# Hybrid encoder layer on one core: the up-projection's weight sums formed during the mixers' projection, three more activations fetched ahead of each down stage, and some transfers kept in program order

## The chip, the cores and the metric

The kernel runs on one core of a Trainium2 chip. The metric is device time in microseconds (us) of one execution; the time before is the median of three runs. Beside it stands one execution that the hardware profiler recorded. A core has TensorE (PE, matmuls, with PEld for its weight loads), VectorE (DVE), ScalarE (ACT), GpSimd (POOL) and SyncE (SP), which here issues nearly all transfers. Each engine works through its own instructions in order; semaphores tie them together.

## The reference, cut to what matters

One layer is computed for a prompt of 2048 rows and for 8 sample sequences of 16 rows (128 rows), with D = 1024:

```python
h = rms_norm(x, norm_g[0])
z = h @ w_in                                  # 1024 x 3592
att = rms_norm(band_attention(qa, ka, va), g_att)         # 8 heads of 64
mem = sigmoid(ob) * head_norm(mlstm(qb, kb, vb, ib, fb))  # 4 heads of 128
x = x + rms_norm(concat(att, mem) @ w_out, norm_g[1])
u = rms_norm(x, norm_g[2]) @ w_up             # 1024 x 5632
y = causal_depthwise_conv(u, width=3)
ffn = (gelu(y[:, :2816]) * y[:, 2816:]) @ w_down          # 2816 x 1024
x = x + rms_norm(ffn, norm_g[3])
```

All is float32. Outputs are x and the caches and states of both request groups.

## The kernel before, in words

Every float32 product is made of three matmuls (`mm3`, L95 to L97) on operands that ScalarE and VectorE split into a high part (a cast) and a low part (a subtraction). The rows form 17 tiles of 128: 16 of the prompt and one of all samples (SAMPLE).

**The mixers' projection** goes over the tiles twice, as two halves of 9 and 8 tiles. In each half 14 groups of columns of w_in (`GROUPS`, gi = 0 to 13) are multiplied; `group_T` yields after every four of eight k steps (12 steps per group), `group_rows` likewise (two steps per tile: 18 or 16). The loop at L1186 takes these steps one by one. In each it also takes a step of whatever else is under way, loads and splits of the next group's weights (`load_group`), norms of input rows (`norm_steps`), and calls `pump`, which steps two pipes of units: attention heads and mLSTM heads. [...] The tag "grow" of the pool `const` has one buffer, which holds the input norm's row during the projection, the mix norm's row (`norm_row(1)`) during the output projection, and later the last norm's row.

**The output projection** (`project`) follows, and from tile 8 on the FFN's pools are open.

**The FFN** runs over three blocks of 6, 6 and 5 tiles (`FBLOCKS`, L1387). Its up-projection is a Strassen-Winograd scheme: for each f of 22 (128 gate and 128 up columns), seven products of quarter matrices (`product`, L1395), 84 matmuls. Four of the seven weight operands are sums of the quarters a11, a12, a22 and a21. In block 0, `load_quads` (L1255) loads the four quarters of an f (L1262), forms four sums on GpSimd (L1267, 128×512 each), stores them in DRAM as `wsd[f]` (L1269) and uses the tiles directly; blocks 1 and 2 load three quarters and four kept sums (L1278). `load_up` (L1282) splits each operand (`split`, L1250 and L1251). The raw tiles are "quads", 128×512, of which there are 11 buffers; w_down's raw tiles, the early activations and the `later` units below share them.

Per f the products' results leave PSUM through `x1` to `x3`, `uu` and `ug` (L1403, L1473 to L1492); `conv` makes the convolution with VectorE's L1423 and L1424, and the gated product is stored as `gd[b][f]` (L1501). `conv` and the product use three row buffers (`row`, tag "yq").

**The down stage** of a block goes twice over the 22 f, once per half `dh` of the output columns, here called k; each k has 18 (or 15) matmuls of 128×512. `fetch` (L1438) reads gd[b][k] back, into two quads if `early`, else into a row buffer (L1447); `split_g` (L1449) splits it into two of four "w3" tiles. Activations 0 and 1 are fetched early, at f = 20, and split at f = 21; from there on, each step k fetches k+1. In each step the pipe `ahead` takes a step: the next block's normed and transposed rows (`h2_units`) and the `later` units of the previous block's output tiles (L1353), which load a half row of the FFN's result and of x (L1357, L1358), scale, add and store.

Before block 0, `late_B` (L1131) loads and splits four of the seven row operands.

Of the kernel before, what the change touches and what calls it, by code (L numbers as in the profile page):

```python
# [17 lines left out]
P = 128  # L18
# [26 lines left out]
def hymba_step(ctx: ExitStack, tc: tile.TileContext, I: dict, O: dict):  # L45
# [1085 lines left out]
    def late_B():  # L1131

        for i in (P5, P2, P4, P3):
# [3 lines left out]
            nc.scalar.copy(hi, lo.bitcast(F32))  # L1137
            nc.vector.tensor_tensor(lo, lo.bitcast(F32), hi, op=ALU.subtract)  # L1138

    GROUPS = ["va0", "qk0", "qk1", "va1", "qk2", "qk3", "qb0", "vo0", "qb1", "vo1", "qb2", "vo2", "qb3", "vo3"]  # L1140
    SRC = {g: i for i, g in enumerate(["va0", "qk0", "qk1", "va1", "qk2", "qk3",
                                       "qb0", "vo0", "qb1", "vo1", "qb2", "vo2", "qb3", "vo3"])}
# [24 lines left out]
    def norm_steps(half):  # L1167

        for ci, tiles in enumerate(HALVES[half]):
            ch = phT.tile([P, 2, KT, 384], F32R, tag="hT", name=f"hT{half}_{ci}", bufs=3)  # L1170
            chunks.append(ch)
            for j, t in enumerate(tiles):
                norm_tile(t, ch, j, ps_big)
                yield 0.9, 2.5
# [3 lines left out]
    pipes += [Pipe(att_stream()), Pipe(mem_stream())]  # L1178
    chunks = []
    norms = norm_steps(0)  # L1180
    next(norms)
    pend = load_group(0)
    for _ in pend[2]:
# [2 lines left out]
    for n_, (half, gi) in enumerate(seq):  # L1186
        wh, wl, _ = pend
        split = iter([])
        if n_ + 1 < len(seq):
            pend = load_group(seq[n_ + 1][1])  # L1190
            split = pend[2]
        g = GROUPS[gi]
        i = int(g[2])
        nm = f"{g}_{half}"
        if g[:2] == "va":
            it = group_rows(wh, wl, half, chunks, vd[i], nm, 264 if gi == 0 else 256,
                            [O["v_prompt"][i], O["v_sample"][i].unsqueeze(1)])
        elif g[:2] == "qk":
            it = group_T(wh, wl, half, chunks, [qTd[i], kTd[i]], [-(DA ** -0.5), None], nm,
                         [None, [O["k_prompt"][i], O["k_sample"][i]]])  # L1200
        elif g[:2] == "qb":
            it = group_T(wh, wl, half, chunks, [[t_[:, c, :] for t_ in qkbd[i]] for c in range(2)],
                         [None, DH ** -0.5], nm)
        else:
            it = group_rows(wh, wl, half, chunks, vobd[i], nm)
        if half == 0 and gi == 13:
            chunks = []
            norms = norm_steps(1)
        if n_ == len(seq) - 1:
            out = project([0, 1, 2, 3, 4, 5, 6, 7, SAMPLE, 8, 9, 10, 11, 12, 13, 14, 15])  # L1210
            split = w_out_steps()
            next(split)
            next(out)
        for u, (pe, dve) in enumerate(it):
            ahead = []
            if n_ < len(seq) - 1 or u >= 6:
                ahead.append(next(split, (0.0, 0.0)))
            if n_ == len(seq) - 1 and u == 12:
                ahead.append(next(out))
            if (half == 0 and gi == 13 and u >= 6 and u % 2 == 0) or (gi == 0 and u % 2 == 0):  # L1220
                ahead.append(next(norms, (0.0, 0.0)))
            pump(pe + sum(a[0] for a in ahead), dve + sum(a[1] for a in ahead))
        for _ in split:
            pass
        if gi == 0:
            if half == 0:
                nc.sync.dma_start(bgate, I["b_gate"].broadcast_to([P, 8]))
                nc.sync.dma_start(gatt, I["g_att"])
                heads.append(build_bias)
                mems.append(lambda: prep(prep_sample()))  # L1230
            mems.append(lambda half=half: prep(prep_prompt(half)))
        if g[:2] == "qk":
            attention(i, half)
            if half == 0 and i == 3:
                heads.insert(len(heads) % 4, lambda: attention_sample(0, EARLY))
            if half == 1 and i == 0:
                heads.insert(len(heads) % 4, lambda: attention_sample(EARLY, DB))
        if g[:2] == "vo":
            mems.append(lambda i=i, half=half: mlstm(i, half))
            if half == 0:  # L1240
                mems.append(lambda i=i: mlstm_sample(i))
# [8 lines left out]
        nc.scalar.copy(h, r)  # L1250
        nc.vector.tensor_tensor(l, r, h, op=ALU.subtract)  # L1251

    raws = {}

    def load_quads(b, f, g):  # L1255

        src = lambda i: I["w_up"][f][:, i * 512:(i + 1) * 512]
        if b == 0 and g == 0:
            q = []
            for i in range(4):  # L1260
                q.append(quad(f"wu{f}_{i}"))
                nc.sync.dma_start(q[i], src(i))  # L1262
            a11, a12, a22, a21 = q
            s1, s2, s3, s4 = [quad(f"ws{f}_{i}") for i in range(4)]
            for o, x, y, op in ((s1, a21, a22, ALU.add), (s2, s1, a11, ALU.subtract), (s3, a11, a21, ALU.subtract),
                                (s4, a12, s2, ALU.subtract)):
                nc.gpsimd.tensor_tensor(o, x, y, op=op)  # L1267
            for i, o in enumerate((s2, s3, s1, s4)):
                nc.sync.dma_start(wsd[f][:, i * 512:(i + 1) * 512], o)  # L1269
            raws[f] = [a12, a22, s4]  # L1270
            return [a11, s2, s3, s1]
        if b == 0:
            return raws.pop(f)
        kept = lambda i: wsd[f][:, i * 512:(i + 1) * 512]
        out = []
        for i, s_ in enumerate([[src(0), kept(0), kept(1), kept(2)], [src(1), src(2), kept(3)]][g]):
            r = quad(f"wu{b}_{f}_{g}_{i}")
            nc.sync.dma_start(r, s_)  # L1278
            out.append(r)
        return out  # L1280
# [72 lines left out]
    def later(t, rs):  # L1353

        def unit(half):
            v, x, c = quad(f"f{half}{t}"), quad(f"x{half}{t}"), half * 512
            nc.sync.dma_start(v, (f0d, f1d)[half][t])  # L1357
            nc.sync.dma_start(x, x2d[t][:, c:c + 512])  # L1358
            yield 0.0, 0.0
            nc.vector.scalar_tensor_tensor(v, v, rs, g3[:, c:c + 512], op0=ALU.mult, op1=ALU.mult)  # L1360
            nc.gpsimd.tensor_tensor(v, v, x, op=ALU.add)
            nc.sync.dma_start(out_rows(t)[:, c:c + 512], v)
            yield 0.0, 1.0

        return [unit(half) for half in range(2)]
# [21 lines left out]
    for b, tiles in enumerate(FBLOCKS):  # L1387
# [48 lines left out]
        n2 = nt * P // 2  # L1436

        def fetch(dh, k, early=False):  # L1438
            if k >= NF:
                return  # L1440
            if early:
                g[dh, k] = [quad(f"gr{b}_{dh}_{k}_{i}")[:, :n2] for i in range(2)]
                for i, r in enumerate(g[dh, k]):
                    nc.sync.dma_start(r, gd[b][k][:, i * n2:(i + 1) * n2])
            else:
                g[dh, k] = row(f"gr{b}_{dh}_{k}")
                nc.sync.dma_start(g[dh, k][:, :2 * n2], gd[b][k][:, :2 * n2])  # L1447
# [14 lines left out]
        for f in range(NF):  # L1462
# [20 lines left out]
            if f == NF - 1:  # L1483
                split_g(0, 0, w3_tile)
                split_g(0, 1, w3_tile)
            ug = u_tile(f"ug{nm}")
            product(P2, w[0], a, onto=True)
            nc.scalar.copy(ug[:, 2:2 + n], a[:, :n])
# [18 lines left out]
        for dh in range(2):  # L1507
# [9 lines left out]
            for c in range(6):  # L1517
# [16 lines left out]
                if tail and c >= 4:  # L1534
                    places = []
                    for i in ((0, 1) if c == 4 else (2,)):
                        t_ = p3.tile([P, 2, 4, 384], F32R, tag=f"B{i}", name=f"gtail{i}", bufs=1)
                        t_ = t_.rearrange("p a k n -> p (a k n)")
                        places += [t_[:, x * 768:(x + 1) * 768] for x in range(4)]
                    for k in ks:  # L1540
                        split_g(dh, k, lambda name: places.pop())
                        fetch(dh, k + 1)
                    if c == 4:
                        wh4, wl4 = wh, wl
                        continue
                    for j in range(nt):
                        for k in range(16, 20):
                            down(j, k, wh4, wl4)
                        for k in ks:
                            down(j, k, wh, wl)  # L1550
                        finish(b, j, load_rest(b, j), *evacuate(b, j, accs[j], 1), res[j])
                    continue
                for k in ks:
                    if (dh, k) not in parts:
                        split_g(dh, k, w3_tile)
                    if k + 1 == NF and dh == 0:
                        fetch(1, 0)
                    elif dh == 1 or k >= 1:
                        fetch(dh, k + 1)
                    for j in order if k == NF - 1 else range(nt):  # L1560
                        down(j, k, wh, wl)
                    if k >= 1:
                        ahead.step()
# [115 lines left out]
```

## Time and profile before

| | us |
|---|---|
| median of 3 runs | 2871.17 |
| lowest and highest | 2869.95, 2876.76 |
| profiled execution | 2872.21 |
| its span, first to last instruction | 2870.5 |

| busy in the span | us | share |
|---|---|---|
| PE | 2752.3 | 96% |
| PEld | 2566.0 | 89% |
| DVE | 1899.5 | 66% |
| ACT | 1405.6 | 49% |
| POOL | 561.8 | 20% |

How such lines are read: a group of instructions has its line in the kernel, the engine, the operation, the tiles written and read (out<-in), the shapes and the count; then busy time and the mean of one in ns; then the engine's idle time just before them and what ended it (the releaser). A row of waits has who waited for whom, the total in us, the number of times and the longest. A row of busy times by stretch has the stretch in us from the span's start, its length, the busy us and count of each engine, then PEclk (the granted TensorE clock, 1.00 is full), the DMA engines' busy share and GB/s. A row of the timeline has its start, its duration, the instruction, and in brackets the idle time before it and its releaser. Rows of DMA issues have the count, the size of one and the median time from issue to landing.

### The profile page before, as it was taken

Reading aid. Unit: us, or ns where it says so; the run is one execution under the profiler, and the core shown is the slowest. Engines: PE = TensorE matmul, PEld = TensorE weight load, DVE = VectorE, ACT = ScalarE, POOL = GpSimd, SP = SyncE. Lnnn points to the kernel's source line nnn. Section 1 sums busy time; section 2 is a strip of 40 time slices with the busy share of each in tenths; the row PEclk is TensorE's granted clock in tenths of the full one; section 3 lists DMA queues with packets and bytes.
Section 4 is the critical chain, followed back from the end, with each engine's and each line's share of the span. In section 5 each row is a group of like instructions: output and inputs, shape, how many; then the busy total and the mean of one; then the engine's idle time right before and its main releaser. Section 6 shows DMA issues by size and latency. Waiting matters only on the chain.

```text
span 2870.5 us, 47064 instructions
## 1 busy us (share of the span) xinstructions
PE 2752.3 (96%) x16587; PEld 2566.0 (89%) x16587; DVE 1899.5 (66%) x3345; ACT 1405.6 (49%) x2827; POOL 561.8 (20%) x964
## 2 busy tenths in 40 slices
PE   8899999999999999999999989999999899999898
PEld 7899989989899998878989978899999778999787
DVE  5344455645456678576999976467777754888755
ACT  4344555534356676343444445345554443555433
POOL 1000010211000003255555410011111210222311
PEclk9999999999999999999999999999999999999899
DMA  4544355556555564366444545645444775555766
GB/s 163 171 120 124 110 174 152 177 161 194 169 154 153 157 192 148 106 198 211 152 166 144 167 141 171 217 147 158 148 149 162 235 242 160 171 174 181 234 222 200
DMA packets 312122, 486.04 MB, mean 169 GB/s; under 512 B 55282, under 2 KB 148174, under 8 KB 311758
## 3 DMA queue, kind: packets, MB, share of 16 engines
q1 hardware_dynamic: 273294, 449.21, 50.1%
q10 hardware_dynamic: 38592, 33.83, 3.5%
q8 instruction: 130, 2.13, 0.3%
q14 instruction: 106, 0.87, 0.1%
HBM read 359.36 MB, written 126.70 MB: 169 GB/s over the span
## 4 chain that ended last, share of the span: by engine, by line
PE 49%; DVE 7%; issue 2%; DMA 2%; ACT 1%; POOL 1%; SPq 0%; DVEq 0%; ACTq 0%; POOLq 0%
PE uec L95 5%; PE uec L96 5%; PE uec L97 5%; PE dn L97 4%; PE dn L96 4%; PE dn L95 4%; PE ua L95 3%; PE ua L97 2%; PE ua L96 2%; PE dnm L95 2%; PE dnm L97 2%; PE dnm L96 2%; PE wo L97 2%; PE wo L95 2%; PE wo L96 2%
## 5 line engine op out<-in xcount | busy, mean ns | idle before, releaser
L95 PE MATMUL uec<-B,wuh 128*128 128x384 f32 (+1 forms) x720 | 236.2, 329 | 7.9 <-DVE uu L1490 7.9
L1251 DVE TENSOR_TENSOR gl<-gr,gh 128x768 fp32r<-128x768 f32 (+3 forms) x132 | 117.8, 897 | 188.2 <-ACT gh L1250 188.1
L96 PE MATMUL uec<-B,wuh 128*128 128x384 f32 (+1 forms) x720 | 235.6, 327 | 0.4 <-DVE B L1138 0.4
L97 PE MATMUL uec<-B,wul 128*128 128x384 f32 (+1 forms) x720 | 233.0, 327 | 0.0
L1250 ACT CAST gh<-gr 128x768 fp32r<-128x768 f32 (+3 forms) x132 | 101.5, 773 | 238.2 <-PE dn L96 200.0
L95 PE MATMUL dn<-wdh,gh 128*128 128x512 f32 x466 | 185.1, 397 | 7.9 <-DVE ug L1403 7.9
L96 PE MATMUL dn<-wdl,gh 128*128 128x512 f32 x466 | 185.9, 399 | 0.0
L1251 DVE TENSOR_TENSOR wul<-wu,wuh 128x512 fp32r<-128x512 f32 x255 | 179.3, 742 | 9.4 <-ACT wuh L1250 6.6
L1250 ACT CAST wuh<-wu 128x512 fp32r<-128x512 f32 x255 | 141.6, 617 | 71.3 <-PE uec L96 67.5
L97 PE MATMUL dn<-wdh,gl 128*128 128x512 f32 x466 | 170.4, 398 | 0.0
L96 PE MATMUL vo<-wi_l,hT 128*128 128x256 f32 x544 | 155.7, 286 | 0.0
L95 PE MATMUL vo<-wi_h,hT 128*128 128x256 f32 x544 | 154.9, 285 | 0.6 <-DVE mt L199 0.6
L97 PE MATMUL vo<-wi_h,hT 128*128 128x256 f32 x544 | 155.3, 285 | 0.0
L387 DVE CUSTOM_DVE_ANT_0 tmp<-s,nb 128x640 f32<-128x640 f32 (+4 forms) x128 | 94.3, 737 | 77.1 <-PE s L377 73.6
L95 PEld LDWEIGHTS uec<-B,wuh 128*128 128x128 f32 x720 | 135.4, 188 | 11.0 <-DVE uu L1490 9.8
L96 PEld LDWEIGHTS uec<-B,wuh 128*128 128x128 f32 x720 | 135.5, 188 | 0.9 <-DVE B L1138 0.7
L97 PEld LDWEIGHTS uec<-B,wul 128*128 128x128 f32 x720 | 135.1, 188 | 0.0
L95 PE MATMUL qk<-hT,wi_h 128*128 128x384 f32 (+1 forms) x384 | 128.8, 335 | 4.2 <-ACT qk_st L226 3.6
L95 PE MATMUL dnm<-wdh,gh 128*128 128x512 f32 x252 | 101.8, 407 | 31.6 <-ACT gh L1250 29.8
L388 ACT ACTIVATE tmp<-tmp,mn 128x640 f32<-128x640 f32 (+4 forms) x128 | 97.6, 762 | 70.2 <-DVE mn L387 65.9
L400 DVE TENSOR_TENSOR ptl<-pt,pth 128x640 fp32r<-128x640 f32 (+4 forms) x128 | 93.5, 737 | 55.8 <-ACT pth L399 54.7
L97 PE MATMUL qk<-hT,wi_l 128*128 128x384 f32 (+1 forms) x384 | 128.9, 336 | 0.0
(409 smaller groups left out, 9065.4 us busy)
## 6 DMA issues: line engine op xcount, KB each, us to landing
wu<-in_w_up SPq DMA_DIRECT2D x220, 256.0 KB, 3.8
wu<-wsd SPq DMA_DIRECT2D x176, 256.0 KB, 5.0
wdr<-in_w_down SPq DMA_DIRECT2D x132, 256.0 KB, 4.5
gr<-gd SPq DMA_DIRECT2D x84, 384.0 KB, 3.5
wi_raw<-in_w_in SPq DMA_DIRECT2D x52, 512.0 KB, 4.4
wsd<-ws SPq DMA_DIRECT2D x88, 256.0 KB, 3.2
gd<-g SPq DMA_DIRECT2D x44, 384.0 KB, 2.8
kraw<-kTd SPq DMA_DIRECT2D x112, 128.0 KB, 3.4
```

The source lines that it names most:

```text
L95: nc.tensor.matmul(out, ah, bh, start=start, stop=False, skip_group_check=onto)
L96: nc.tensor.matmul(out, ah, bl, start=False, stop=False, skip_group_check=onto)
L97: nc.tensor.matmul(out, al, bh, start=False, stop=stop, skip_group_check=onto)
L387: nc.vector.tensor_tensor_reduce(o_, s_, b_, 1.0, 3e38, ALU.add, ALU.min, accum_out=mn)
L388: nc.scalar.activation(tmp[:, :n], tmp[:, :n], AF.Exp, bias=mn, scale=-1.0, accum_out=rsum[:, i % 4, hh:hh + 1])
L400: nc.vector.tensor_tensor(s.ptl[:, sl, qc], ptv, s.pth[:, sl, qc], op=ALU.subtract)
L1250: nc.scalar.copy(h, r)
L1251: nc.vector.tensor_tensor(l, r, h, op=ALU.subtract)
```

## The change: what it does

1. **The sums.** `sum_steps` makes all 22 f's weight sums during the projection: 44 units, each of half the columns. A unit loads a 128×4×256 tile (512 KB) into the "grow" buffer, takes three steps, makes four additions in place on GpSimd (128×256), takes two steps, stores the tile into wsd, and takes two more. The loop takes one step of it in each step of groups 2 to 12 of the first half and 1 to 12 of the second; a unit under way is finished at the start of group 13. Its loads and stores go through `keep_in_program_order`, which puts an instruction behind the one traced before it on the same engine. As "grow" is needed by it, the input norm's row is loaded again for the second half (`g0.clear()`).
2. **The loads.** `load_quads` no longer forms sums: all three blocks load four and three quads per f, three quarters and four kept sums, in wsd's new order.
3. **The `later` units' loads** (L1357, L1358) are kept in program order too.
4. **Early fetches.** At f = 21 of every block, after activations 0 and 1 are split, activations 2, 3 and 4 are fetched early, into quads. From there on each step k of the down stage fetches k+2 instead of k+1, and the last steps of the first half fetch activations 0 and 1 of the second.

```diff
+    def sum_steps():
+        for f in range(NF):
+            for e in range(2):
+                view = lambda t: t.rearrange("p (q c) -> p q c", q=4)[:, :, e * 256:(e + 1) * 256]
+                w = const.tile([P, 4, 256], F32, tag="grow", name=f"ws{f}_{e}")
+                tc.keep_in_program_order(nc.sync.dma_start(w, view(I["w_up"][f])))
+                for _ in range(3):
+                    yield True
+                a11, a12, a22, a21 = [w[:, i] for i in range(4)]
+                nc.gpsimd.tensor_tensor(a22, a21, a22, op=ALU.add)
+                nc.gpsimd.tensor_tensor(a21, a11, a21, op=ALU.subtract)
+                nc.gpsimd.tensor_tensor(a11, a22, a11, op=ALU.subtract)
+                nc.gpsimd.tensor_tensor(a12, a12, a11, op=ALU.subtract)
+                for _ in range(2):
+                    yield True
+                tc.keep_in_program_order(nc.sync.dma_start(view(wsd[f]), w))
+                yield True
+                yield False
...
+    sums, under_way = sum_steps(), False
...
         if half == 0 and gi == 13:
             chunks = []
             norms = norm_steps(1)
+            g0.clear()
...
+            if 2 - half <= gi < 13:
+                under_way = next(sums, False)
+            while gi == 13 and under_way:
+                under_way = next(sums)
             pump(pe + sum(a[0] for a in ahead), dve + sum(a[1] for a in ahead))
...
-        src = lambda i: I["w_up"][f][:, i * 512:(i + 1) * 512]
-        if b == 0 and g == 0:
-            q = []
-            for i in range(4):
-                q.append(quad(f"wu{f}_{i}"))
-                nc.sync.dma_start(q[i], src(i))
-            a11, a12, a22, a21 = q
-            s1, s2, s3, s4 = [quad(f"ws{f}_{i}") for i in range(4)]
-            for o, x, y, op in ((s1, a21, a22, ALU.add), (s2, s1, a11, ALU.subtract), (s3, a11, a21, ALU.subtract),
-                                (s4, a12, s2, ALU.subtract)):
-                nc.gpsimd.tensor_tensor(o, x, y, op=op)
-            for i, o in enumerate((s2, s3, s1, s4)):
-                nc.sync.dma_start(wsd[f][:, i * 512:(i + 1) * 512], o)
-            raws[f] = [a12, a22, s4]
-            return [a11, s2, s3, s1]
-        if b == 0:
-            return raws.pop(f)
+        own = lambda i: I["w_up"][f][:, i * 512:(i + 1) * 512]
         kept = lambda i: wsd[f][:, i * 512:(i + 1) * 512]
         out = []
-        for i, s_ in enumerate([[src(0), kept(0), kept(1), kept(2)], [src(1), src(2), kept(3)]][g]):
+        for i, s_ in enumerate([[own(0), kept(0), kept(3), kept(2)], [own(1), own(2), kept(1)]][g]):
...
-            nc.sync.dma_start(v, (f0d, f1d)[half][t])
-            nc.sync.dma_start(x, x2d[t][:, c:c + 512])
+            tc.keep_in_program_order(nc.sync.dma_start(v, (f0d, f1d)[half][t]))
+            tc.keep_in_program_order(nc.sync.dma_start(x, x2d[t][:, c:c + 512]))
...
-            if k >= NF:
+            if dh > 1 or k >= NF:
...
                 split_g(0, 1, w3_tile)
+                for k in range(2, 5):
+                    fetch(0, k, True)
...
                         split_g(dh, k, lambda name: places.pop())
-                        fetch(dh, k + 1)
+                        fetch(dh, k + 2)
...
-                    if k + 1 == NF and dh == 0:
-                        fetch(1, 0)
-                    elif dh == 1 or k >= 1:
-                        fetch(dh, k + 1)
+                    if dh == 1 or k >= 3:
+                        fetch(dh + (k + 2) // NF, (k + 2) % NF)
```

More of the change, by code (lines that the diff above doesn't have):

```diff
@@ L1251, in split @@
         nc.vector.tensor_tensor(l, r, h, op=ALU.subtract)
-    raws = {}
     def load_quads(b, f, g):
-        src = lambda i: I["w_up"][f][:, i * 512:(i + 1) * 512]
-        if b == 0 and g == 0:
-            q = []
-            for i in range(4):
-                q.append(quad(f"wu{f}_{i}"))
-                nc.sync.dma_start(q[i], src(i))
-            a11, a12, a22, a21 = q
-            s1, s2, s3, s4 = [quad(f"ws{f}_{i}") for i in range(4)]
-            for o, x, y, op in ((s1, a21, a22, ALU.add), (s2, s1, a11, ALU.subtract), (s3, a11, a21, ALU.subtract),
-                                (s4, a12, s2, ALU.subtract)):
-                nc.gpsimd.tensor_tensor(o, x, y, op=op)
-            for i, o in enumerate((s2, s3, s1, s4)):
-                nc.sync.dma_start(wsd[f][:, i * 512:(i + 1) * 512], o)
-            raws[f] = [a12, a22, s4]
-            return [a11, s2, s3, s1]
-        if b == 0:
-            return raws.pop(f)
+        own = lambda i: I["w_up"][f][:, i * 512:(i + 1) * 512]
         kept = lambda i: wsd[f][:, i * 512:(i + 1) * 512]
         out = []
-        for i, s_ in enumerate([[src(0), kept(0), kept(1), kept(2)], [src(1), src(2), kept(3)]][g]):
+        for i, s_ in enumerate([[own(0), kept(0), kept(3), kept(2)], [own(1), own(2), kept(1)]][g]):
             r = quad(f"wu{b}_{f}_{g}_{i}")
```

## The prediction

> **What bounds the kernel now.** I read the head of the page first, then busy time by stretch, cut where the stages change, then TensorE's own waits in the stretches that lose time.
>
> ```profile
> span 2870.5 us, 47064 instructions
> ## 1 busy us (share of the span) xinstructions
> PE 2752.3 (96%) x16587; PEld 2566.0 (89%) x16587; DVE 1899.5 (66%) x3345; ACT 1405.6 (49%) x2827; POOL 561.8 (20%) x964
> ```
> ```profile
> core 0: us, PE busy (x) PEld busy (x) DVE busy (x) ACT busy (x) POOL busy (x), PEclk, DMA share, GB/s
> ...
> 50.00:1150.00 1100.00, 1071.93 (x7572) 1033.75 (x7571) 619.11 (x1518) 576.96 (x1408) 109.89 (x300) 0.99 0.52 156
> 1331.20:1694.10 362.90, 340.65 (x1873) 328.99 (x1872) 333.55 (x382) 170.40 (x274) 183.11 (x174) 0.99 0.50 164
> 1895.50:2218.70 323.20, 322.67 (x1843) 320.93 (x1841) 248.91 (x368) 161.69 (x264) 44.08 (x94) 1.00 0.49 153
> 1694.10:1712.40 18.30, 7.33 (x24) 5.52 (x24) 10.36 (x12) 7.63 (x12) 2.01 (x5) 0.72 0.47 157
> 2218.70:2242.00 23.30, 10.18 (x28) 7.70 (x28) 12.47 (x14) 7.94 (x13) 5.13 (x8) 0.63 0.48 167
> 2698.40:2719.80 21.40, 7.75 (x20) 5.59 (x20) 14.30 (x19) 5.31 (x8) 7.37 (x7) 0.60 0.95 327
> 2800.00:2850.00 50.00, 50.00 (x218) 40.80 (x217) 22.42 (x31) 20.25 (x34) 0.44 (x2) 1.00 0.62 203
> ```
>
> TensorE bounds the whole; a gain can come only from places where it stands or runs at a low clock. The second row is the mixers' projection (28.1 us idle of 1100). The third and fourth are the up stages of FFN blocks 0 and 1: nearly the same matmuls, 1873 in 362.9 us against 1843 in 323.2 us. At block 1's 0.1754 us each, block 0's would take 328.3 us: it loses **34.6 us**. The next three rows are the first microseconds of the three down stages: 63.0 us for 72 matmuls, at clocks 0.60 to 0.72. The last row is a down stage at full pace, 50/218 = 0.23 us each, so 72 need 16.6 us: **46.4 us** lost. Together 81 us lie in what the diff touches.
>
> TensorE's waits, first in block 0's up stage, then at the three changes to a down stage:
>
> ```profile
> PE ua L95 <- ACT wuh L1250: 9.4, 7, 1.9
> PE uec L95 <- DVE uu L1490: 9.2, 10, 1.7
> ```
> ```profile
> PE dnm L95 <- ACT gh L1250: 10.3, 1, 10.3
> ```
> ```profile
> PE dnm L95 <- ACT gh L1250: 8.9, 1, 8.9
> PE dn L95 <- DVE ug L1403: 4.2, 1, 4.2
> ```
> ```profile
> PE dnm L95 <- ACT gh L1250: 10.6, 1, 10.6
> PE dn L95 <- DVE ug L1403: 3.1, 1, 3.1
> ```
>
> **Block 0's up stage: minus 30 us.** Only block 0 forms the weight sums, four additions per f on GpSimd (L1267). VectorE is busy 333.55 of 362.9 us there against 248.91 in block 1, for the same work and late_B. The groups of VectorE show why, block 0 (250 us of it), then block 1:
>
> ```profile
> L1251 DVE TENSOR_TENSOR wul<-ws,wuh 128x512 fp32r<-128x512 f32 x41 | 45.8, 1137 | 0.0
> ...
> L1477 DVE TENSOR_TENSOR x<-x,uec 128x384 f32<-128x384 f32 x15 | 8.2, 543 | 1.7 <-PE uec L97 1.7
> ```
> ```profile
> L1251 DVE TENSOR_TENSOR wul<-wu,wuh 128x512 fp32r<-128x512 f32 x81 | 52.1, 684 | 0.0
> ...
> L1477 DVE TENSOR_TENSOR x<-x,uec 128x384 f32<-128x384 f32 x17 | 9.4, 554 | 11.2 <-PE uec L97 11.2
> ```
> ```profile
> L1267 POOL TENSOR_TENSOR ws<-wu,wu 128x512 f32<-128x512 f32 x42 | 67.6, 1608 | 62.5 <-DMA wu<-in_w_up 48.8 <-DVE wul L1251 10.1 <-DVE x L1477 3.2
> L1267 POOL TENSOR_TENSOR ws<-wu,ws 128x512 f32<-128x512 f32 x21 | 37.8, 1799 | 0.0
> L1267 POOL TENSOR_TENSOR ws<-ws,wu 128x512 f32<-128x512 f32 x21 | 37.1, 1765 | 1.6
> ```
>
> The split's subtraction takes 1137 ns beside the sums and 684 ns without; the subtraction that reads PSUM is no slower (543 against 554). So 142.5 us of GpSimd sums stretch VectorE until it, not TensorE, paces the stage. After the change block 0 runs the very instructions of block 1, where VectorE has a quarter of its time free and TensorE never waits. Its DMAs per f go from four loads and four stores to seven loads of 256 KB, as in block 1. What stays is the start: late_B.
>
> ```profile
> 1341.14 8.51 DVE L1138 TENSOR_TENSOR B<-B 128x1536 fp32r<-128x1536 f32 x4
> ```
> ```profile
> 1350.31 0.45 PE L97 MATMUL ua<-B,wul 128*128 128x384 f32 x1 [2.27 <-DVE wul L1251]
> ...
> 1351.20 0.52 PE L97 MATMUL ua<-B,wul 128*128 128x384 f32 x1
> 1351.52 0.52 PE L95 MATMUL ua<-B,wuh 128*128 128x384 f32 x1
> ```
>
> VectorE is held 8.5 us, TensorE then waits 2.3 us, and matmuls follow at 0.32 us instead of 0.175. I leave 4.6 of the 34.6 us there: −30. Bounds: −34.6, and −17 if only the waits above without the clock's part (9.4 + 9.2) go, less the start.
>
> **Changes to the down stages: minus 38 us.** Where the first hold comes from, at block 0, from SyncE's queue and ScalarE, with the two halves of an early activation ahead:
>
> ```profile
> 1701.20 0.32 SPq L1501 DMA_DIRECT2D gd<-g  x1
> 1701.58 24.19 SPq L1447 DMA_DIRECT2D gr<-gd  x8
> ```
> ```profile
> 1675.19 0.93 ACT L1250 CAST gh<-gr 128x384 fp32r<-128x384 f32 x2 [0.47 <-PE uec L96]
> ...
> 1707.30 0.83 ACT L1250 CAST gh<-gr 128x768 fp32r<-128x768 f32 x1 [1.65 <-DMA gr<-gd]
> ```
>
> Activation 2 is fetched (L1447) into a row buffer that f=21's convolution still holds, so its transfer starts behind the last gd store at 1701.58, and TensorE, through with k=0 and 1, stands 10.3 us. The change puts k=2 to 4 into quad buffers while f=21 multiplies. Three activations are 3×18 matmuls×0.23 = 12.4 us of work. Activation 5, the next in a row buffer, still goes out at about 1701.6, lands as k=2 did (cast at 1707.3), and is wanted at 1697.7 + 12.4 = 1710: covered by some 2 us. The quads suffice: 4 for w_down and 6 for activations, of 11, once k=0 and 1 are split.
>
> The second hold (4.2 and 3.1 us) is a transfer that came ahead of its place, here in block 1:
>
> ```profile
> 2220.78 0.75 DVE L1360 SCALAR_TENSOR_TENSOR f<-f,drs,norm_row 128x512 f32<-128x512 f32 x1 [3.85 <-DMA f<-f1d]
> ...
> 2222.38 0.55 DVE L1403 TENSOR_TENSOR ug<-x,uec 128x384 f32<-128x384 f32 x1
> ```
>
> An f of the previous block's output held VectorE 3.85 us ahead of the ug that frees PSUM. L1357 and L1358, kept in program order, come only in the down stage.
>
> Late next: k=2's split needs the w3 tiles of k=0, free six matmuls (1.4 us) before TensorE is through with k=1; the first half's cast and difference take about 0.5 us each. With the wait for ug I leave 2.2 us per change: 46.4 − 6.6 = 39.8. Holding back f and x loads the other way: the last block's first 12 steps of k need about 14.8 MB (24 f and x loads, 12 output stores, ten activations, eight w_down quads), 45 us at the 327 GB/s above, against 41 of matmuls: +2. So −38; bounds −46.4 and −7 (only the ug waits).
>
> The row at 1350 bears on the leftovers: a gap of 2.3 us was followed by about 3 us at half pace. [...]
>
> **The projection: plus 9 us.** There 44 loads, 176 additions of 128×256, 44 stores (512 KB each way, in runs of 1 KB) and one more norm row are added. Nearest rows, the last two from block 0's up stage and the projection:
>
> ```profile
> wi_raw<-in_w_in SPq DMA_DIRECT2D x52, 512.0 KB, 4.4
> ...
> x2d<-mx SPq DMA_DIRECT2D x17, 512.0 KB, 2.9
> ```
> ```profile
> L97 PE MATMUL vo<-wi_h,hT x544: 276/281/384, 259.2 to 1055.5; 128*128 128x256 f32 x182
> ```
> ```profile
> SPq L1269 <- POOL ws L1267: 152.4, 59, 8.8
> ```
> ```profile
> POOL nb L320 <- DMA nb<-relrow: 456.6, 16, 78.3
> ```
>
> The loop's 396 steps fill some 1055 us, 2.7 us each; 316 of them may carry sums and 44×7 = 308 are needed. Load 4.4 us against three steps (8.0); four additions, each half of L1267's 1.6 to 1.8 us, 3.4 us against two (5.3); store 2.9 us against two, before the one buffer is loaded again. GpSimd rises from 110 to about 250 of 1100 us, VectorE by at most what block 0 showed over block 1 (333.55 − 248.91 less late_B's 8.5: 76 us, on 619), and 46.1 MB raise the DMA share from 0.52 to about 0.66. TensorE stays the bound. But latencies grow: its 28.1 us idle by about the DMA's quarter, 7 us, and 2 for queues, +9. Bounds: 0 (also for less than nothing: 28 idle in all), and 38, a third of what SyncE would be held if each of 44 stores waited the 2.6 us that L1269's did. Behind such a store stand head and weight loads, which ScalarE's casts wait for; behind a sum that waits for its load stand, on GpSimd, the mask on mb and the pow for which VectorE's head norm waits. I take 9, near the low end, since the steps leave 1.9 us or more at each link.
>
> **Sum:** −30 − 38 + 9 = −59. The profiled execution took 2872.2 us (span 2870.5 and 1.7 around it), 1.0 above the median of 2871.2: 2872.2 − 59 − 1 = **2812 us**, own range 2795 to 2830.
>
> **Rivals.** *The projection pays*: pinned stores hold SyncE at the upper bound, 38 instead of 9: 2841. For it: GpSimd waited 456.6 us behind nb's DMA, so its queue does stand; against: SyncE's other DMAs may still be moved ahead. Chance 0.20. *The early fetch is not early*: other SyncE waits in the last f keep k=2 behind the last gd store; −7 instead of −38: 2843. Against it: gd of f=2 to 4 was stored long before, and quads free in time. 0.08. *Slower*: a sum lands on GpSimd behind nb's memset, 456.6/16 = 28.5 us a time, the pinned store then holds every load on SyncE; against a gain of 68 this decides from three such holds that reach TensorE; four give 2871 − 68 + 114 = 2917. 0.05. *All of it*: −34.6 − 46.4, nothing paid: 2790. 0.10. Forecast 0.57.
>
> **Range** 2790 to 2850 leaves out the slower case and the tails of two others. Within 0.3% (8.6 us, about what a measurement tells from no change) falls only a part of the first rival: 0.03. Slower 0.05, faster 0.92.
>
> **What would show it.** Right: block 0's up stage near 330 us, its L1251 at 684 ns with no L1267; no hold above 2 us at the three changes, gr transfers ahead of the last gd store; no f ahead of ug; projection's TensorE idle below 40 us. Wrong: SyncE waiting on GpSimd for microseconds in the projection, ScalarE's waits for wi_raw, kraw or mvo growing, or k=5 as the new late activation.

## The result, and the profile after

| kernel | median us | lowest, highest | ratio to the kernel before, 95% interval |
|---|---|---|---|
| before, beside it | 2870.56 | 2867.26, 2876.76 | 1 |
| changed | 2908.89 | 2906.55, 2915.41 | 1.0135 [1.0111, 1.0158] |

The changed kernel is slower by 38 us; the forecast was 59 us faster. The profiled execution took 2906.55 us. Its page begins:

```profile
span 2904.8 us, 47380 instructions
## 1 busy us (share of the span) xinstructions
PE 2771.9 (95%) x16587; PEld 2575.7 (89%) x16587; DVE 1841.9 (63%) x3354; ACT 1412.9 (49%) x2836; POOL 552.2 (19%) x1052
```

TensorE is still busy for 95% and VectorE has 58 us less to do, so the totals hide the matter. Busy time by stretch shows it. The stretches are the first half of the projection, its tail (no matmul of the second half yet), the second half, and the output projection, up to the FFN's first matmul. The first block is before, the second after, where one more stretch is needed (545 to 632):

```profile
core 0: us, PE busy (x) PEld busy (x) DVE busy (x) ACT busy (x) POOL busy (x), PEclk, DMA share, GB/s
0.00:489.00 489.00, 460.87 (x3193) 450.26 (x3194) 236.97 (x559) 233.16 (x534) 25.70 (x94) 0.99 0.48 145
489.00:530.00 41.00, 41.00 (x354) 41.00 (x353) 24.72 (x42) 25.59 (x56) 6.70 (x16) 1.00 0.48 151
530.00:1057.00 527.00, 515.02 (x3749) 498.00 (x3749) 309.33 (x800) 283.42 (x706) 59.07 (x178) 0.99 0.57 168
1057.00:1331.20 274.20, 265.81 (x1413) 222.72 (x1413) 189.34 (x296) 130.91 (x314) 105.30 (x137) 0.99 0.50 159
```
```profile
0.00:505.00 505.00, 469.58 (x3187) 455.64 (x3188) 240.25 (x554) 230.50 (x529) 78.76 (x162) 0.98 0.58 174
505.00:545.00 40.00, 39.37 (x333) 38.80 (x331) 18.65 (x43) 21.41 (x50) 7.80 (x19) 1.00 0.50 145
545.00:632.00 87.00, 47.63 (x174) 36.96 (x175) 42.78 (x134) 26.81 (x86) 31.25 (x74) 0.53 0.57 172
632.00:1141.00 509.00, 488.40 (x3549) 471.21 (x3547) 281.18 (x645) 259.84 (x608) 107.78 (x204) 1.00 0.65 199
1141.00:1435.40 294.40, 277.03 (x1465) 228.92 (x1466) 197.69 (x322) 138.28 (x335) 99.60 (x139) 0.99 0.49 154
```

The FFN begins at 1435.4 instead of 1331.2: **104 us are lost ahead of it**. From there to the end it takes 2904.8 − 1435.4 = 1469.4 us instead of 2870.5 − 1331.2 = 1539.3: **70 us are won**. The row to look at is the third: 87 us between the halves of the projection in which TensorE has 174 matmuls, at half its clock. But the others lose as well. The first row has six matmuls fewer than before in 16 us more, at a DMA share of 0.58 instead of 0.48.

The FFN does what was forecast. Block 0 from the first up matmul to the first down matmul, before and after, and after's split:

```profile
1331.26:1683.89 352.63, 330.40 (x1826) 320.44 (x1824) 326.10 (x372) 166.56 (x268) 182.05 (x172) 0.99 0.51 166
```
```profile
1435.54:1755.33 319.79, 318.29 (x1825) 317.65 (x1824) 254.14 (x372) 168.70 (x268) 42.47 (x87) 1.00 0.52 166
```
```profile
L1277 DVE TENSOR_TENSOR wul<-wu,wuh 128x512 fp32r<-128x512 f32 x103 | 66.1, 684 | 0.0
```

32.8 us are gone and the subtraction takes 684 ns as in block 1. TensorE's waits in the whole FFN after, where the three changes to a down stage alone had held it 10.3, 8.9 and 10.6 us:

```profile
PE dnm L95 <- ACT gh L1276: 5.7, 5, 2.4
...
PE dn L95 <- DVE ug L1411: 2.6, 3, 1.3
```

Two of these five waits for gh come early in the last down stage, 0.7 us for activation 5 and 2.4 us for activation 6. SyncE's, ScalarE's and TensorE's rows:

```profile
2753.72 0.32 SPq L1511 DMA_DIRECT2D gd<-g  x1
2754.10 0.42 SPq L1455 DMA_DIRECT2D gr<-gd  x1
```
```profile
2757.27 0.72 ACT L1276 CAST gh<-gr 128x640 fp32r<-128x640 f32 x1 [5.55 <-DMA gr<-gd]
```
```profile
2758.05 0.50 PE L95 MATMUL dnm<-wdh,gh 128*128 128x512 f32 x1 [0.73 <-ACT gh L1276]
...
2764.47 0.50 PE L95 MATMUL dnm<-wdh,gh 128*128 128x512 f32 x1 [2.45 <-ACT gh L1276]
```

Activation 5, the first in a row buffer, goes out just behind the last gd store, and ScalarE stands 5.55 us until it lands.

So the fault lies in the projection. What stood in the hole at 545 us? SyncE's transfers there, with the sums' stores (L1156) and loads (L1146):

```profile
594.09 0.56 SPq L1156 DMA_DIRECT2D wsd<-ws  x1
...
597.46 0.55 SPq L1146 DMA_DIRECT2D ws<-in_w_up  x1
...
604.84 0.57 SPq L1156 DMA_DIRECT2D wsd<-ws  x1
...
608.30 0.55 SPq L1146 DMA_DIRECT2D ws<-in_w_up  x1
...
617.56 0.56 SPq L1156 DMA_DIRECT2D wsd<-ws  x1
...
621.19 0.35 SPq L89 DMA_DIRECT2D norm_row<-in_norm_g  x1
...
630.34 0.33 SPq L212 DMA_DIRECT2D xr<-in_x_prompt  x1
```

and VectorE's first norm of the second half, with what ended its wait:

```profile
625.84 2.48 DVE L219 SCALAR_TENSOR_TENSOR xr<-xr,n_rs,norm_row 128x1024 f32<-128x1024 f32 x2 [0.32 <-DMA norm_row<-in_norm_g]
```

The first half's last sums are still being made at 617 us. They hold "grow", the only buffer of its tag, and the second half's norms need the gain row in that very buffer (`g0.clear()`, L1230). Until it is there no row of the second half is normed, and no matmul of its projection can start. Before, the row stayed where it was and these norms ran from 505 to 546 us.

### The profile page after: what moved, and what is told of

It reads as the page before. It is cut to its first block, busy times and chain, and to the rows that moved or that the text cites. A ratio compares the mean times of both kernels' runs of the same rounds, so it can differ in the third digit from the quotient of the medians.

```text
span 2904.8 us, 47380 instructions
## 1 busy us (share of the span) xinstructions
PE 2771.9 (95%) x16587; PEld 2575.7 (89%) x16587; DVE 1841.9 (63%) x3354; ACT 1412.9 (49%) x2836; POOL 552.2 (19%) x1052
## 4 chain that ended last, share of the span: by engine, by line
PE 51%; DMA 2%; DVE 1%; ACT 1%; issue 1%; POOL 0%; SPq 0%; ACTq 0%; DVEq 0%; POOLq 0%
PE uec L95 6%; PE uec L96 6%; PE uec L97 6%; PE dn L97 3%; PE dn L96 3%; PE dn L95 3%; PE ua L97 3%; PE ua L96 3%; PE ua L95 3%; PE dnm L95 2%; PE dnm L97 2%; PE dnm L96 2%; PE ub L96 1%; PE ub L97 1%; PE ub L95 1%; PE wo L95 1%
## 5 line engine op out<-in xcount | busy, mean ns | idle before, releaser
L1277 DVE TENSOR_TENSOR gl<-gr,gh 128x768 fp32r<-128x768 f32 (+3 forms) x141 | 117.9, 844 | 158.7 <-ACT gh L1276 158.2
L1276 ACT CAST wuh<-wu 128x512 fp32r<-128x512 f32 x315 | 173.0, 617 | 78.4 <-PE uec L96 74.4
L1277 DVE TENSOR_TENSOR wul<-wu,wuh 128x512 fp32r<-128x512 f32 x315 | 201.8, 683 | 2.8 <-DMA x2d<-mx 2.8
L1276 ACT CAST wu<-wu 128x512 fp32r<-128x512 f32 x147 | 84.7, 617 | 98.9 <-PE uec L96 64.0
```

## Experiments

**Theory 1** is that buffer. **Theory 2** is that the added work slows the whole projection: 2a by its bytes, 2b by the waits it puts into SyncE's queue, 2c by the waits it puts into GpSimd's, 2d by the additions beside VectorE. **Theory 3** says why the sums are late: the tie to program order. Differences below are those of the ratios times 2868.5 us, about the median of before beside these runs.

### e1: the second half without the gain row

```diff
-        nc.vector.scalar_tensor_tensor(xr, xr, rs, g0[0], op0=ALU.mult, op1=ALU.mult)
+        nc.vector.scalar_tensor_tensor(xr, xr, rs, xr if 8 <= t < SAMPLE else g0[0], op0=ALU.mult, op1=ALU.mult)
...
-            g0.clear()
```

> The changed kernel, but the second half's input norm doesn't use the gain row: its VectorE multiplication takes the row of x itself in the gain's place (the same operation on the same shapes, so the second half's numbers differ), and the row isn't loaded again. Theory 1 (the gain row shares its one buffer with the sums, so the second half's norms stand behind the last sum of the first half): the hole from 545 to 632 us closes; 87 us less about 26 us of pipe matmuls that were worked off in it at half clock and now come back (174 at 0.15 us) is 61, so about 2846 us, 2830 to 2860. Theory 2 (the sums' transfers and GpSimd additions slow the whole projection by contention): no more than 10 us less, 2895 or above.

2879.94 us, 1.0037 [1.0024, 1.0050]. The hole is gone: the second half's first matmul starts at 554 us instead of 632. But only 28 us are won of the 61 expected, and the kernel is still slower than before. Theory 1 is true and explains about a quarter of the 104 us lost ahead of the FFN; theory 2 is left with the rest. The time lies between the two expectations.

### e2: the sums' transfers without the tie

```diff
-                tc.keep_in_program_order(nc.sync.dma_start(w, view(I["w_up"][f])))
+                nc.sync.dma_start(w, view(I["w_up"][f]))
...
-                tc.keep_in_program_order(nc.sync.dma_start(view(wsd[f]), w))
+                nc.sync.dma_start(view(wsd[f]), w)
```

> The changed kernel with the sums' loads and stores free of the tie to program order; the buffer is still shared. Theory 1 with theory 3 (the sums are late because each of their transfers is tied behind the mixers' transfers traced ahead of it): the last sum of the first half is stored near 505 us, the hole closes, about 2846 us. Theory 1 without theory 3 (late for another reason, such as the pace of six waits per unit): 2900 to 2910. Theory 2: 2900 to 2915.

2886.93 us, 1.0065 [1.0043, 1.0086]: 20 us less than the changed kernel, and at none of the expected times. SyncE's timeline and waits (up to the FFN):

```profile
347.49 0.56 SPq L1156 DMA_DIRECT2D wsd<-ws  x1
...
351.10 0.33 SPq L89 DMA_DIRECT2D norm_row<-in_norm_g  x1
```
```profile
SPq L1156 <- POOL ws L1153: 80.5, 32, 5.2
SPq L1146 <- DMA wsd<-ws: 78.5, 37, 4.1
...
SPq L1156 <- DMA ws<-in_w_up: 33.4, 17, 3.9
```

The first half's last sum is stored at 347 instead of 617 us and the gain row follows at once: theory 3 holds, the tie made the sums late. But the same sums, no longer held back, now follow each other closely, and SyncE waits 192 us for them in the two halves. TensorE reaches the second half at 574 us, against 530 before and 554 in e1. Of the 28 us that the hole costs, 20 come back here; the other 8, not far outside what the intervals leave open, are paid in another place.

### e3: the sums end early in the first half

```diff
-                for _ in range(3):
+                for _ in range(2):
                     yield True
...
-                for _ in range(2):
-                    yield True
+                yield True
...
-            if 2 - half <= gi < 13:
+            if 2 - half <= gi < (8, 13)[half]:
                 under_way = next(sums, False)
-            while gi == 13 and under_way:
+            while gi == (8, 13)[half] and under_way:
```

> The changed kernel with five steps per unit of sums in place of seven, and the first half's sums ending at group 8 of 14 instead of 13; pins and shared buffer stay. Theory 1: with the end some 150 us earlier in the program, even sums 130 us late are through when the second half's norms want the row; the hole closes, 2840 to 2865 (a few us may be lost to the tighter pace). Theory 2: the same transfers in fewer steps, 2905 to 2930.

2892.53 us, 1.0078 [1.0063, 1.0093]: outside both expectations. The gain row is loaded at 399 us and the second half starts at 545, so the hole is gone, as theory 1 says; the time is 12 us above e1, which keeps the pace of seven steps. With e1 and e2 this settles that the hole is real and is not the main thing.

### e4, e10, e11: the down stage's edits alone

e10 is the kernel before with only this edit:

```diff
-            nc.sync.dma_start(v, (f0d, f1d)[half][t])
-            nc.sync.dma_start(x, x2d[t][:, c:c + 512])
+            tc.keep_in_program_order(nc.sync.dma_start(v, (f0d, f1d)[half][t]))
+            tc.keep_in_program_order(nc.sync.dma_start(x, x2d[t][:, c:c + 512]))
```

e11 has only the changed lines of `fetch` and its calls:

```diff
+                for k in range(2, 5):
+                    fetch(0, k, True)
...
-                        fetch(dh, k + 1)
+                        fetch(dh, k + 2)
```

e4 has both; the sums stay in block 0 in all three.

> The kernel before with the down-stage edits alone: f and x loads of the later stage kept in program order, activations 2 to 4 fetched during f=21; the sums stay in block 0's up stage. The prediction's term for this part: -38 (bounds -46.4 and -7), so about 2833 us. If the gain of 70 in the FFN came from the up stage alone: 2865 to 2871. Block 0 holds more quads here than in the changed kernel, so its own change may keep its hold of 10 us: 2843.

> The kernel before with the f and x loads of the later stage kept in program order, nothing else. The prediction's term: the waits for ug at the changes after blocks 1 and 2 (4.2 and 3.1 us) go, with the slow clock behind them: about -9, 2858 us (2852 to 2867). If the loads held back make the later stage late instead: 2867 or above.

> The kernel before with activations 2 to 4 fetched during f=21 and the next ones two steps ahead, nothing else. The prediction's term: the holds for gh (10.3, 8.9 and 10.6 us) go with the slow clock behind them, about -28, 2839 us (2832 to 2850). If e4's 35 us came only with both edits together: less than 15 us won, 2852 or above.

| | median us | ratio, 95% interval | won |
|---|---|---|---|
| e4, both | 2832.95 | 0.9870 [0.9854, 0.9886] | 37.3 |
| e11, early fetch | 2841.99 | 0.9906 [0.9891, 0.9921] | 27.0 |
| e10, order of f and x | 2864.86 | 0.9989 [0.9980, 0.9998] | 3.2 |

TensorE's waits in e4 at the change in block 0, where 10.3 us had stood:

```profile
PE dn L95 <- DVE ug L1403: 0.6, 1, 0.6
PE dnm L95 <- ACT wdh L1250: 0.5, 1, 0.5
```

The fear that block 0's extra quads would keep the hold there was wrong. All three times fit what was expected from the prediction's terms, e10 near the edge of its range. Together the edits win 7 us more than the sum of each alone, about as much as the three intervals leave open. The waits don't explain it: TensorE's waits for ug in the FFN, 7.9 us before, are 2.1 in e10, 2.6 in e11 and 2.5 in e4, so they go with either edit alone. **e4 beats both the kernel before and the changed one.**

### e12: the sums alone

The changed kernel with e4's edits taken back.

> The changed kernel without the two edits of the down stage: only the sums are moved. If the parts add up (e4: -35): 2909 + 35 = 2944 us, 2938 to 2950, so the move of the sums alone costs 75. If the down-stage edits gain less in the changed kernel than by themselves: below 2935.

2943.09 us, 1.0261 [1.0247, 1.0275]: slower than before by 75, and by the ratios 36 above the changed kernel, where e4 had won 37. The parts add up.

### e5, e9: the bytes alone

From here on the base is e1, so that the hole takes no part; like it, these kernels leave something out and don't compute the layer. In e5 each unit of sums is one transfer, in e9 two, three steps apart:

```diff
-                tc.keep_in_program_order(nc.sync.dma_start(w, view(I["w_up"][f])))
+                tc.keep_in_program_order(nc.sync.dma_start(view(wsd[f]), view(I["w_up"][f])))
                 for _ in range(3):
                     yield True
+                tc.keep_in_program_order(nc.sync.dma_start(view(wse[f]), view(I["w_up"][f])))
```

> The kernel without the gain row for the second half (2880 us), in which each unit of sums is one transfer of 512 KB from w_up straight to wsd, DRAM to DRAM: the load, the additions and the store are left out, so the bytes are moved but SyncE never waits for a buffer and GpSimd does nothing (the weight sums are wrong). With no cost in the projection at all the time would be 2868 less the 70 us that the FFN gained: about 2798. Theory 2a (traffic: the added bytes lengthen all other transfers): 2860 to 2880. Theory 2b (SyncE, an in-order queue, is held by each sum's load, waiting for the last store, and each store, waiting for the additions or the load; e1's trace shows 53.8 and 53.1 us): 2800 to 2815. Theory 2c (GpSimd: its queue stands at the first addition until the load lands, 363.8 us in e1, and other GpSimd work behind it is late): also 2800 to 2815.

> e5 with two DRAM-to-DRAM transfers of 512 KB per unit in place of one, three steps apart, the second into a DRAM tensor that nothing reads: as many bytes through the DMA engines as the changed kernel's load and store, and still nothing that SyncE waits for, no additions. e5 cost +22 us ahead of the FFN, e8 (load and store, no additions) +49. If the bytes alone make e8's time (2a): about 2850. If it is SyncE's waits (2b): about 2826 to 2832.

e5 took 2826.25 us, 0.9859 [0.9838, 0.9879]; e9 2838.31 us, 0.9891 [0.9878, 0.9905]. If the projection cost nothing, 2868.5 − 70 = 2798.5 would be seen (the 70 is from two profiled executions; e4's 37.3 and block 0's 32.8 make as much). So the bytes of a load and a store cost some 39 us, with no instruction waiting for a sum. Both results lie between their expectations. The same 1000 us of the projection, before and in e9:

```profile
50.00:1050.00 1000.00, 973.57 (x6973) 948.21 (x6972) 535.85 (x1342) 509.92 (x1234) 80.86 (x252) 0.99 0.52 154
```
```profile
50.00:1050.00 1000.00, 955.08 (x6767) 927.95 (x6768) 514.10 (x1295) 489.06 (x1186) 84.78 (x246) 0.99 0.65 195
```

At 0.65 the DMA engines are far from full, yet TensorE's idle time rises from 26.4 to 44.9 us and 206 matmuls fewer are done. One way by which it gets there shows in the transfers of the projection's own weights. Their median from issue to landing was 4.4 us before; in e9 it is 5.4:

```profile
wi_raw<-in_w_in SPq DMA_DIRECT2D x52, 512.0 KB, 5.4
```

and ScalarE waits longer for them, before and in e9:

```profile
ACT wi_h L1161 <- DMA wi_raw<-in_w_in: 31.9, 20, 4.1
```
```profile
ACT wi_h L1176 <- DMA wi_raw<-in_w_in: 42.0, 19, 5.4
```

A transfer from DRAM to DRAM isn't a load and a store; that the engines carry as much is read from the share, 0.65 here and 0.63 in e8 below. Nor are the 39 us the bytes alone: e9 also puts 88 more issues into SyncE's queue, of some 0.55 us each if they take what the sums' issues take in the changed kernel's rows above, and the order of the other work may change with them. No run parts these.

### e8: load and store, no additions

```diff
-                nc.gpsimd.tensor_tensor(a22, a21, a22, op=ALU.add)
-                nc.gpsimd.tensor_tensor(a21, a11, a21, op=ALU.subtract)
-                nc.gpsimd.tensor_tensor(a11, a22, a11, op=ALU.subtract)
-                nc.gpsimd.tensor_tensor(a12, a12, a11, op=ALU.subtract)
```

> The same base with load and store of each unit on SyncE as in the changed kernel and the four additions left out, so that the store waits for the load alone. Theory 2c: GpSimd's waits are gone, 2800 to 2815. Theories 2a and 2b: nearly nothing is won, 2865 to 2880, as the loads still wait for the stores and the bytes are the same.

2852.69 us, 0.9947 [0.9929, 0.9965]: neither expectation, between them. Against e9 it has nearly the same bytes, and SyncE waits, with a load until the last store has freed the buffer and with a store (L1151 here) until the load has landed:

```profile
50.00:1050.00 1000.00, 942.12 (x6615) 912.85 (x6614) 507.31 (x1278) 480.88 (x1166) 82.78 (x244) 0.98 0.63 192
```
```profile
SPq L1146 <- DMA wsd<-ws: 50.9, 26, 4.7
...
SPq L1151 <- DMA ws<-in_w_up: 44.2, 24, 4.0
```

These 95 us of SyncE (96 with smaller rows) cost 16 us of time, and 152 more matmuls are missing from the stretch.

### e6 and e13: the additions' work

e6 has the additions on one tile and no transfers; e13 is e8 with four subtractions per unit on a tile that nothing else uses:

```diff
+                for _ in range(4):
+                    tc.keep_in_program_order(nc.gpsimd.tensor_tensor(spare, spare, spare, op=ALU.subtract))
```

> The same base, with the additions alone: one load at the start, then 176 additions of 128x256 on the same tile at the same places; no other transfer for the sums, and the FFN loads w_up's own quadrants in place of the sums (same sizes, wrong values). Theories 2a and 2b: 2798 to 2810. A fourth possibility, 2d (the additions themselves, 130 us of GpSimd beside VectorE, stretch VectorE's operations): 2820 or above. Theory 2c in its waiting form: 2798 to 2810, as nothing is waited for.

> e8 (load and store of each unit, no additions; 2853 us) with four subtractions of 128x256 per unit put back at their place in the program, on a spare tile of GpSimd's own: they wait for no load, and no store waits for them (the weight sums are wrong). e1, with the additions tied to both transfers, took 2880. Theory 2c (waiting: GpSimd's queue stands in front of each first addition until its load lands, and SyncE's store until the last addition is done): 2853 to 2863. Theory 2d (the work of the additions itself, beside VectorE): 2872 to 2882.

e6 took 2808.38 us, 0.9802 [0.9780, 0.9824]: 13 us above the 2798.5 by the ratios, and in the range against 2d. But it isn't the test that it was meant to be: with nothing to wait for, the additions all ran one after another, from 48 to 228 us. e13 keeps them at their places: 2857.99 us, 0.9964 [0.9949, 0.9978], as 2c's waiting form expected. That is 5 us above e8 with the intervals overlapping, and 21 below e1, which has the same bytes and the same number of additions but ties them together. The operations are not quite equal: one takes 613 ns in e13, where it reads a single tile, and 737 in e1. So 2d as the main cost falls and the waiting form holds. VectorE's split of the projection's weights, before and in e13:

```profile
L1162 DVE TENSOR_TENSOR wi_l<-wi_raw,wi_h 128x512 fp32r<-128x512 f32 x100 | 65.5, 689 | 36.9 <-ACT wi_h L1161 36.5
```
```profile
L1182 DVE TENSOR_TENSOR wi_l<-wi_raw,wi_h 128x512 fp32r<-128x512 f32 x100 | 68.3, 716 | 60.8 <-ACT wi_h L1181 60.4
```

It is stretched from 689 to 716 ns, while block 0's dense sums had stretched the like from 684 to 1137. In e6, from 48 to 228 us, it took 951 ns beside dense additions of the same 128×256, against 686 there before:

```profile
L1182 DVE TENSOR_TENSOR wi_l<-wi_raw,wi_h 128x512 fp32r<-128x512 f32 x20 | 18.3, 951 | 12.9 <-ACT wi_h L1181 12.8
```

How much is lost goes in these rows with how closely GpSimd's operations follow each other: 951 ns in e6, where the additions filled 76.16 of the 100 us from 100 to 200, and 716 in e13, where GpSimd was busy for 194.45 us of the 1000 in all.

What the ties do is seen in SyncE's and GpSimd's waits of the same 1000 us, SyncE's in e13 first, then e1's:

```profile
SPq L1156 <- DMA ws<-in_w_up: 58.8, 23, 6.5
SPq L1149 <- DMA wsd<-ws: 48.5, 27, 4.6
```
```profile
SPq L1146 <- DMA wsd<-ws: 53.8, 25, 4.8
SPq L1156 <- POOL ws L1153: 50.9, 21, 3.8
...
SPq L1156 <- DMA ws<-in_w_up: 14.7, 7, 3.4
```
```profile
POOL ws L1150 <- DMA ws<-in_w_up: 359.2, 36, 32.0
```
```profile
50.00:1050.00 1000.00, 929.84 (x6425) 894.54 (x6425) 500.52 (x1222) 460.42 (x1115) 208.47 (x400) 0.97 0.61 185
```

With the smaller rows of the same two lines, SyncE's waits at the sums' loads and stores rise from 109 us in e13 to 134, while GpSimd's queue, which stood for no sum in e13, stands at the first addition of a unit for 359 us. (The profiled execution of e1 took 2888.55 us, 8.6 above its median.) In e8 96 us of SyncE's waits had cost 16, so 26 more would hardly make 21: GpSimd's queue probably has a part. e7 bears on it.

### e7: the sums' transfers in GpSimd's queue

```diff
-                tc.keep_in_program_order(nc.sync.dma_start(w, view(I["w_up"][f])))
+                tc.keep_in_program_order(nc.gpsimd.dma_start(w, view(I["w_up"][f])))
```

and the store likewise.

> The same base with the sums' loads and stores issued from GpSimd's own queue instead of SyncE's; the bytes and additions stay. Theory 2b: SyncE is free, 2800 to 2825. Theory 2a: 2870 to 2885, as before. Theory 2c: as slow or slower, 2880 to 2920, since GpSimd now also issues and waits.

2863.70 us, 0.9991 [0.9976, 1.0006]: 13 us less than e1, in none of the three ranges. SyncE is free of the sums, GpSimd takes their waits, here again in the same 1000 us:

```profile
POOL ws L1150 <- DMA ws<-in_w_up: 186.5, 42, 7.6
...
POOL ws L1146 <- DMA wsd<-ws: 107.1, 30, 6.6
```

Of the 42 us that e1 stands above e9, 29 are still there with no wait for a sum in SyncE's queue, so SyncE's waits alone don't make the cost of the tied chain. As GpSimd issues the transfers too here, and waits for the buffer, how e1's 21 us split between the queues stays open. 13 us came back; of the 67 us by the ratios that stay above 0.9756 (before less the FFN's 70), e9's 39 are more than half. SyncE was rid of both its 134 us of waits for the sums and 88 issues of some 0.56 us, and these runs don't tell which of the two was worth the 13.

## Why the prediction was wrong, step by step

**Block 0's up stage, −30.** Right: 32.8 us, by the mechanism given; L1277 at 684 ns, GpSimd's additions gone, TensorE busy 318.29 of 319.79 us.

**The down stages, −38.** Right: e4 gives −37.3. The early fetch is −27.0 of the −28 that its holds were worth. The order of the f and x loads, put at −9 in the expectation, gives −3.2 alone, and 7 more come only with both edits, for a reason that no run shows; that the whole came so near −38 is in part luck. Activation 5 did become the next late one, a sign that the prediction had named, but only in the last block, where 5 and 6 hold TensorE 3.2 us, one of them longer than the 2 us set as the limit; all five waits for gh in the FFN make 5.7 us.

**The projection, +9.** Wrong, and it alone turned the sign. The step that failed reads: "TensorE stays the bound. But latencies grow: its 28.1 us idle by about the DMA's quarter, 7 us, and 2 for queues, +9." In its place the runs put the following, each rung taken away in turn:

| what is added | run | ratio | us |
|---|---|---|---|
| nothing in the projection (before less the FFN's 70, worked out) | | 0.9756 | |
| the bytes, with their 88 issues on SyncE | e9 | 0.9891 | 39 |
| SyncE's waits for the one buffer and for the load | e8 | 0.9947 | 16 |
| the additions' own work | e13 | 0.9964 | 5 |
| additions and transfers tied together | e1 | 1.0037 | 21 |
| the gain row behind the last sum | changed kernel | 1.0135 | 28 |
| sum | | | 109 |

The ratios' intervals are worth 4 to 7 us each, so the 5 is not told from nothing; the other rungs are apart. The start of the FFN in the five profiles gives the same picture: 1367.1, 1380.5, 1388.4, 1416.0 and 1435.5 us after 1331.3, steps of 36, 13, 8, 28 and 19; that the last two are 21 and 28 by the medians goes with e1's profiled execution being 8.6 us above its median. A rung belongs to this order of taking things away.

Three errors made the 9:

- **A missing term, 28 us.** The prediction counted the "one more norm row" as a transfer. It did not ask whose buffer the row takes, nor when the last sum would give it back; and it placed the sums in time by the program's steps, though the tie makes them as late as the mixers' transfers traced ahead of them.
- **The bytes, 39 us and not 7.** Scaling TensorE's idle time by the DMA share takes the wait as proportional to traffic already there. The weights' transfers took 5.4 instead of 4.4 us, and ScalarE's waits for any transfer rose from 181 to 216 us of the 1000: transfers that had just been hidden are hidden no more. How much of the 39 comes this way, and how much from the added issues, is not shown.
- **The waits, 37 us and not 2.** The rival "the projection pays" had 38 for this, a third of what SyncE would be held if each of 44 stores waited 2.6 us, 114 us in all. e1's SyncE was held 134 us and the two rungs are 16 + 21: the upper bound had the right size, in part by luck. Only 80 of the 134 us were stores'; the rest were loads waiting for the buffer, which it left out. And 26 us more of SyncE's waits came with the 21, which leaves a part to GpSimd's queue, not in that price. The reason given for the low end, that the steps leave 1.9 us or more at each link, failed: loads and stores both waited.

The rival on the slower side had the sign right and the mechanism wrong: it needed holds of 28.5 us behind nb's memset, and SyncE's longest wait at a sum's store was 6.1 us in the changed kernel. That its 2917 lies near 2909 is luck. Of the signs listed, "SyncE waiting on GpSimd for microseconds in the projection" and ScalarE's longer waits for wi_raw both came.

## What to carry to other kernels

When a change borrows a buffer, list every other user of it and ask who gets it next and when the borrower is through in the trace's time, not in the program's. Where an engine is busy for 97% of a stage and transfers are just hidden behind it, as TensorE is in the projection, price added transfers even where the DMA engines have room: 46 MB more, with their 88 issues, cost 39 us here at a DMA share of 0.65, more than the 33 us that moving the sums could win. And price a tied chain of load, compute and store by the waits that it puts into every queue it passes: SyncE's 96 us of them cost 16 here, and tying GpSimd's additions in cost 21 more.

## What the runs showed of the hardware that was not expected

In the hole between the halves TensorE was busy for 47.63 of 87 us, in short pieces, and the granted clock was 0.53: being busy for half of the time did not keep the clock. A transfer of 512 KB from DRAM to DRAM took a median of 6.3 us in e5, beside 5.3 for the load and 4.0 for the store in e8.
